# One step of a two-layer delta-rule and pooling decoder: memory keys moved to the front, x scaled before its split, ScalarE evictions, and a finer weave

## The chip, the core and the metric

The kernel is one program on one core of a Trainium2 chip. The metric is device time in microseconds (us) from the first to the last instruction of the program, as the median of several runs; one more execution was taken with the hardware profiler, and all rows below come from it. The engines are PE (TensorE, matrix products, 128x128 array), DVE (VectorE), ACT (ScalarE), POOL (GpSimd) and SP (SyncE, which here only issues transfers). SBUF is the on-chip memory with 128 partitions, PSUM the eight banks into which PE writes.

## The reference, cut to what matters

A prompt of 256 tokens and eight decode sequences of four tokens (288 columns together) go through two layers, all in float32. Layer 0 mixes with a gated delta rule of 12 heads, layer 1 with causal pooling; each also has four heads that attend to 256 memory tokens. Then comes a dense SwiGLU feed-forward network. The parts that the change touches:

```
def rmsnorm(x, w):
    y = xf * lax.rsqrt(jnp.mean(xf * xf, axis=-1, keepdims=True) + EPS)
    return (y * w).astype(x.dtype)

mkv = [mem_kv(mem_prompt, norm_mem[l], w_mem_kv[l]) for l in range(DEPTH)]   # memory keys and values
h = rmsnorm(x, norm_mix[l])
proj = h @ w_in                                   # q|k|v, z, a, b, q_mem of layer 0
qkv, conv_new = causal_conv(qkv, conv_buf, conv_w)            # width 4, then silu
# delta rule, in chunks: lmat is strictly lower triangular, (eye + lmat) is solved
sol = lax.linalg.triangular_solve(eye + lmat, rhs, left_side=True, lower=True, unit_diagonal=True)
u = uv_c - wk_c @ S;  o = qg_c @ S + attn_c @ u;  S = S * gend_c + kend_c^T @ u
o = rmsnorm(o, onorm_w) * jax.nn.silu(z)
y_mem = cross_attn(q_mem, mem_k[l], mem_v[l])
x = x + jnp.concatenate([y_tok, y_mem], axis=-1) @ w_out[l]
x = x + swiglu(rmsnorm(x, norm_ffn[l]), w_gate_up[l], w_down[l])
```

## The kernel before

Activations lie transposed: 16 blocks of 128 features by 288 tokens. Every large product is made from two halves of each operand: `split` writes a rounded part `hi` (ACT) and the rest `lo` (DVE, `lo = src - hi`), and PE multiplies hi by hi, hi by lo and lo by hi. Weights come from DRAM in chunks of 512 KB through three `wraw` buffers (`wchunk`, L114), ACT makes `whi` (L130) and DVE `wlo` (L131) in pieces of 512 columns. `gemm_steps` (L144) is a generator: each step takes one chunk, which is 24 products of 128x128 by 288 columns, and collects up to four output blocks in the four `acc` banks of PSUM. When a block is done, `on_block` takes it out. Everything else that PE writes goes to four `aux` banks.

A framework records the instructions and orders them: program order gives the priority, and a simulated schedule made ahead of time picks, for each engine, the ready instruction of the highest priority. At run time each engine's queue is in order, and an instruction that waits holds all behind it. `tc.high_priority` moves an instruction ahead.

The stages follow one another so: x and the first key and query projection (`first = kq(0)`, L1154), with x's blocks (`x_block`) loaded between its chunks; then the constants, the rows of x for its norm (`x_norm`, L347, through `wraw` buffers), and the gates (`alpha_beta`, `rates`, `decays`). Since the norm of x comes late, x is split unscaled, and each projection is multiplied by the row `rs0` when it leaves PSUM, on DVE (L667, L670, L652, L714). Then the memory keys and values of layer 0 (`mem_kv`, L271; 192 products of 128x128 by 512 columns). Then six units of two heads each. `Unit.keys` makes the triangular inverse of a unit in levels of 2, 4, 8, 16, 32 and 64 (L848 to L943), `Unit.values` (L975) applies it, updates the states and normalizes. `drain(*gens)` (L476) takes one step of each generator in turn, so that the steps of `values(n)`, `keys(n + 1)`, the memory attention and the projections of the next units alternate: one step of the delta rule, one whole chunk. After that come the output projection (`out_proj`), the feed-forward network (`ffn`), layer 1 (`mix1`) with its own `mem_kv` and `attention`, its output projection, and the second `ffn`.

In `attention`, each pair of decode sequences copies its four probabilities' columns into a zero-padded tile `pad` (L454, POOL) from which PE multiplies (L457); `pad` has one set of columns for both values of b.

Of the kernel before, what the change touches and what calls it, by code (L numbers as in the profile page):

```python
# [16 lines left out]
P = 128  # L17
# [8 lines left out]
TS = 4  # L26
# [19 lines left out]
FILL = 48  # L46
# [6 lines left out]
def VZ(n):  # L53
    return [24 + 2 * n, 25 + 2 * n] + ([36 + 2 * n, 37 + 2 * n] if n < 5 else [])
# [3 lines left out]
def body(ctx: ExitStack, tc: tile.TileContext, i: dict, o: dict):  # L58
# [14 lines left out]

    def acc():
        return accp.tile([P, 512], F32, name="acc", tag="acc", bufs=4)
# [9 lines left out]
    nc.sync.dma_start(cols[:, :32], i["cols"][:, :32])  # L85
# [58 lines left out]
    def gemm_steps(chunk, ncols, kt, act, on_block, ks=2, order=None, bank=None, parts=1):  # L144
# [4 lines left out]
        for k0 in order:  # L149
            nk = min(ks, kt - k0)  # L150
            w = wchunk(chunk(k0 // ks), nk, ncols, parts=parts if k0 == 0 else 1)
            last = k0 == order[-1]
            kj = [(k, j) for k in range(nk) for j in range(nb)]
            for k, j in sorted(kj, key=lambda t: t[1]) if last else kj:
# [4 lines left out]
                en = last and k == nk - 1  # L159
                nc.tensor.matmul(pv, wh, xh, start=st, stop=False)  # L160
                nc.tensor.matmul(pv, wh, xl, start=False, stop=False)  # L161
                nc.tensor.matmul(pv, wl, xh, start=False, stop=en)  # L162
                if en:
                    on_block(j, pv)
            yield
# [14 lines left out]
    class Norm:  # L180
# [25 lines left out]
        def rstd(self):  # L206
            ps = aux()
            for t in range(3):
                rows = P if t < 2 else NS
                nc.tensor.matmul(  # L210
# [19 lines left out]
    def spread_psum(r):  # L230

        ps = aux()
        for t in range(3):
            rows = P if t < 2 else NS
            nc.tensor.matmul(  # L235
# [8 lines left out]
    def row_squares(src, rows, out):  # L244

        for h in range(2):
            t = wpool.tile([P, 1024], F32, name="rows", tag="wraw", bufs=3)[:rows]
            nc.sync.dma_start(t, src[:, h * 1024 : (h + 1) * 1024])
            nc.scalar.activation(t, t, AF.Square, accum_out=out[:rows, h : h + 1])

    def mem_norm():
        q = sp.tile([P, 2, 2], F32, name="mq", tag="mq", bufs=1)
        for t in range(2):
            row_squares(i["mr"][t * P : (t + 1) * P], P, q[:, t])
        mss = small(2, "mss", bufs=1)
        nc.vector.tensor_tensor(mss, q[:, :, 0], q[:, :, 1], op=ALU.add)
# [14 lines left out]
    def mem_kv(l, mem, part_tile, half, kt_, v_):  # L271
        mt = []
        pss = [[acc() for _ in range(2)] for _ in range(2)]
        for k0 in range(0, KT, 2):
            for k in (k0, k0 + 1):
                mt.append(split(mem(k), memw(l, k), hi=part_tile(), lo=part_tile()))
            for part in range(2):
                w = wchunk(i["wkv"][l, part, k0 // 2], 2, 512)
                for t in range(2):
                    for k in range(2):  # L280
# [5 lines left out]
                        nc.tensor.matmul(pv, xh, w[k][0], start=st, stop=False)  # L286
                        nc.tensor.matmul(pv, xl, w[k][0], start=False, stop=False)
                        nc.tensor.matmul(pv, xh, w[k][1], start=False, stop=en)  # L288
                yield
        for t in range(2):  # L290
# [11 lines left out]
            for h in range(NMH):  # L302
                nc.tensor.transpose(
# [8 lines left out]
    pad = cp.tile([P, 2, NMH, 2 * SHIFT + TS], F32, name="pad")  # L312
# [26 lines left out]
    rs0 = sp.tile([P, NT], F32, name="rs0", tag="rs0", bufs=1)  # L339

    def load_constants():
        nc.sync.dma_start(ident, i["ident"])
        nc.sync.dma_start(masks, i["masks"])
        nc.sync.dma_start(levels, i["levels"])
        nc.sync.dma_start(cols[:, 32:], i["cols"][:, 32:])

    def x_norm():  # L347
        q = sp.tile([P, 3, 2], F32, name="xq", tag="xq", bufs=1)
        for t in range(3):
            rows = P if t < 2 else NS  # L350
            row_squares(i["xr"][t * P : t * P + rows], rows, q[:, t])
        ss = small(3, "xss", bufs=1)
        nc.vector.tensor_tensor(ss[:, :2], q[:, :2, 0], q[:, :2, 1], op=ALU.add)
        nc.vector.tensor_tensor(ss[:NS, 2:], q[:NS, 2:, 0], q[:NS, 2:, 1], op=ALU.add)
# [3 lines left out]
    def attention(l, ys, g2, s4, ahead):  # L358
        y = ys[NH:]
        for h in range(NMH):  # L360
            ps = aux()
            pv = ps.rearrange("p (t m) -> p t m", t=2)
            for t in range(2):
                nc.tensor.matmul(
# [13 lines left out]
            for t in range(2):  # L378
                nc.vector.tensor_scalar(e[:, t, :], e[:, t, :], sm[:, t : t + 1], None, op0=ALU.mult)
            pt = aux()  # L380
            ptv = pt.rearrange("p (m t) -> p m t", m=2)
            for m in range(2):
                for t in range(2):
                    nc.tensor.transpose(
# [3 lines left out]
            nc.vector.tensor_copy(pT, ptv)  # L388
            po = aux()
            for m in range(2):  # L390
                nc.tensor.matmul(
# [4 lines left out]
            yield  # L396
# [19 lines left out]
        for b0 in range(0, B, 2):  # L416
            ps = aux()
            for b in (b0, b0 + 1):
                ktb = loaded.pop(0)
                fetch()  # L420
                for h in range(NMH):
                    nc.gpsimd.tensor_copy(
                        pad[:, b % 2, h, SHIFT : SHIFT + TS],
                        y[h][:, NP + b * TS : NP + (b + 1) * TS],
                    )
                for h in range(NMH):
                    nc.tensor.matmul(
                        ps[32 * h : 32 * h + 32, :NM], pad[:, b % 2, h, cols(b)], ktb[:, h, :],
# [1143 lines left out]
```

## Time and profile before

| | us |
|---|---|
| median of three runs (2725.65 to 2731.15) | 2729.69 |
| the profiled execution | 2727.26 |
| its span | 2725.5 |
| PE busy in it | 2657.4 (98%) |
| DVE / ACT / POOL busy | 1593.0 / 1237.9 / 316.5 |

The time of the profiled execution is 1.8 us more than its span. PE's busy time counts pipelined products whose ends are modelled, so it tells where PE had nothing to do, and not how fast it ran; for that the column of the granted clock is read, which is 1.00 at 2.4 GHz and 0.50 at 1.2 GHz.

### The profile page before, as it was taken

The numbers are of one execution on the slowest core, as the hardware profiler recorded it, in microseconds if no ns is written. First come the engines' busy times: TensorE is split into PE (matmuls) and PEld (weight loads), VectorE is DVE, ScalarE is ACT, GpSimd is POOL, SyncE is SP. The second block draws the span as 40 slices with busy tenths as digits, with TensorE's granted clock in tenths as the row PEclk, the third lists the DMA queues.
The fourth block names the chain that finished last, engine by engine and source line by source line (L and its number), as shares of the span: only waits on it lengthen the run. The fifth ranks groups of instructions, "written<-read, shape, count | busy, mean of one in ns | idle before, by whom it ended". The sixth has DMA issues, their size and how long they took to land. (4 is left out here: it accounts for less than half of the span.)

```text
span 2725.5 us, 54445 instructions
## 1 busy us (share of the span) xinstructions
PE 2657.4 (98%) x21400; PEld 2571.2 (94%) x21400; DVE 1593.0 (58%) x3178; ACT 1237.9 (45%) x2407; POOL 316.5 (12%) x620
## 2 busy tenths in 40 slices
PE   7899999999999999999999999999999999999998
PEld 6888888788999999999999988899999999999997
DVE  5558776777655555445555566766555544555544
ACT  5454444444544444344444454455444433444443
POOL 0103221221101000000010111111001000001000
PEclk8999999999999999999999999999999999999998
DMA  7374345434545445455554575655455544545453
GB/s 255 122 233 134 102 151 171 143 118 169 164 164 169 167 166 168 165 169 165 170 166 167 166 248 160 216 174 162 164 170 164 169 167 166 167 166 170 164 170 128
DMA packets 133424, 455.86 MB, mean 167 GB/s; under 512 B 19440, under 2 KB 22000, under 8 KB 133168
## 3 DMA queue, kind: packets, MB, share of 16 engines
q1 hardware_dynamic: 133168, 452.38, 50.1%
q8 instruction: 168, 2.75, 0.4%
q14 instruction: 88, 0.72, 0.1%
HBM read 439.46 MB, written 12.86 MB: 166 GB/s over the span
## 5 line engine op out<-in xcount | busy, mean ns | idle before, releaser
L131 DVE TENSOR_TENSOR wlo<-wraw,whi 128x512 fp32r<-128x512 f32 (+1 forms) x1548 | 1066.6, 696 | 976.7 <-ACT whi L130 946.7
L130 ACT CAST whi<-wraw 128x512 fp32r<-128x512 f32 (+1 forms) x1548 | 939.7, 614 | 1214.2 <-PE acc L161 1128.4
L160 PE MATMUL acc<-a,whi 128*128 128x288 f32 x4864 | 1445.0, 297 | 19.0 <-ACT whi L130 19.0
L162 PE MATMUL acc<-a,wlo 128*128 128x288 f32 x4864 | 1443.8, 297 | 0.0
L161 PE MATMUL acc<-a,whi 128*128 128x288 f32 x4864 | 1443.4, 297 | 0.0
L160 PEld LDWEIGHTS acc<-a,whi 128*128 128x128 f32 x4864 | 918.6, 189 | 24.8 <-ACT whi L130 20.2
L162 PEld LDWEIGHTS acc<-a,wlo 128*128 128x128 f32 x4864 | 918.2, 189 | 5.6 <-issue 2.4
L161 PEld LDWEIGHTS acc<-a,whi 128*128 128x128 f32 x4864 | 918.9, 189 | 3.9 <-issue 1.4
L160 PE MATMUL acc<-b,whi 128*128 128x288 f32 x960 | 282.3, 294 | 0.0
L162 PE MATMUL acc<-b,wlo 128*128 128x288 f32 x960 | 282.3, 294 | 0.0
L161 PE MATMUL acc<-b,whi 128*128 128x288 f32 x960 | 282.3, 294 | 0.0
L1227 POOL TENSOR_TENSOR b<-b,rrow 128x288 f32<-128x288 f32 x88 | 89.4, 1034 | 1259.8 <-ACT b L1226 1259.8
L160 PEld LDWEIGHTS acc<-b,whi 128*128 128x128 f32 x960 | 180.1, 188 | 0.0
L162 PEld LDWEIGHTS acc<-b,wlo 128*128 128x128 f32 x960 | 180.1, 188 | 0.0
L161 PEld LDWEIGHTS acc<-b,whi 128*128 128x128 f32 x960 | 180.1, 188 | 0.0
L195 POOL TENSOR_TENSOR ssum<-ssum,sq 128x288 f32<-128x288 f32 x56 | 53.0, 947 | 427.6 <-ACT sq L194 425.6
L286 PE MATMUL acc<-whi,a 128*128 128x512 f32 x128 | 50.9, 406 | 5.1 <-ACT a L174 5.1
L288 PE MATMUL acc<-wlo,a 128*128 128x512 f32 x128 | 50.2, 393 | 0.0
L1225 DVE TENSOR_TENSOR b<-acc,rrow 128x288 f32<-128x288 f32 x88 | 40.1, 456 | 16.1 <-PE acc L162 16.1
L1226 ACT ACTIVATE b<-b 128x288 f32<-128x288 f32 x88 | 36.6, 439 | 26.1 <-DVE b L1225 25.8
L1231 DVE TENSOR_TENSOR b<-acc,b 128x288 f32<-128x288 f32 x88 | 39.9, 454 | 1.6
L690 DVE SCALAR_TENSOR_TENSOR ckq<-xp,cols,ckq 128x312 f32<-128x312 f32 x72 | 37.2, 547 | 0.7 <-ACT ckq L688 0.5
(378 smaller groups left out, 1607.0 us busy)
## 6 DMA issues: line engine op xcount, KB each, us to landing
wraw<-in_wgu_dram SPq DMA_DIRECT2D x352, 512.0 KB, 3.3
wraw<-in_wdn_dram SPq DMA_DIRECT2D x176, 512.0 KB, 3.2
wraw<-in_w_dram SPq DMA_DIRECT2D x103, 512.0 KB, 3.7
wraw<-in_wout_dram SPq DMA_DIRECT2D x64, 512.0 KB, 3.3
wraw<-in_wkv_dram SPq DMA_DIRECT2D x32, 512.0 KB, 4.2
wraw<-in_w1u_dram SPq DMA_DIRECT2D x32, 384.0 KB, 3.2
s<-in_dS_dram SPq DMA_DIRECT2D x12, 512.0 KB, 4.8
out_dram<-s SPq DMA_DIRECT2D x12, 512.0 KB, 3.8
```

The costliest lines, as they stand in the source:

```text
L130: nc.scalar.copy(hi[:, :n], src)
L131: nc.vector.tensor_tensor(lo[:, :n], src, hi[:, :n].bitcast(F32), op=ALU.subtract)
L160: nc.tensor.matmul(pv, wh, xh, start=st, stop=False)
L161: nc.tensor.matmul(pv, wh, xl, start=False, stop=False)
L162: nc.tensor.matmul(pv, wl, xh, start=False, stop=en)
L195: nc.gpsimd.tensor_tensor(self.sum, self.sum, q, op=ALU.add)
L286: nc.tensor.matmul(pv, xh, w[k][0], start=st, stop=False)
L288: nc.tensor.matmul(pv, xh, w[k][1], start=False, stop=en)
L690: nc.vector.scalar_tensor_tensor(c[:, :312], xp[:, q : q + 312], convw(q, f), c[:, :312], op0=ALU.mult, op1=ALU.add,)
L1225: nc.vector.tensor_tensor(t, ps, rs, op=ALU.mult)
L1227: nc.gpsimd.tensor_tensor(t, t, rs, op=ALU.mult)
L1231: nc.vector.tensor_tensor(t, ps, t, op=ALU.mult)
```

## The change

Five things, with much renaming around them (`nc.tensor.matmul` becomes `mm`).

1. The order at the start. `mem_kv` of layer 0 runs first; x's rows, x's blocks, the memory's rows (`mem_norm`), the constants and the gates are placed between its steps. The rows go through buffers of their own (`gp`, four of 256 KB) instead of `wraw`.
2. `rs0` is ready before x is split, so `x_block` multiplies x by it, and the projections leave PSUM by a plain copy on ACT (z straight through Silu).
3. Further work moves from DVE to ACT: the keys' transposes, the scaling of v, part of the output's, the last copy of the inverse, the scaling and the copy of the attention's probabilities.
4. The eight `copy_predicated` on 32 partitions at the start of each inverse become four of double width; for that `la` of both halves is one tile.
5. `gemm_steps` yields twice in a chunk. `Lane` and `weave` take the place of `drain(*gens)`: the number that a generator yields is how many half chunks pass before its next step. z gets projections of its own, which are moved to later units; ten half chunks of the output projection are the filler of the last unit. In `values` the four state multiplies on POOL stand behind the state's products; `pad` gets a second set.

```
-    def drain(*gens):
-        live = list(gens)
-        while live:
-            for g in list(live):
-                if next(g, live) is live:
-                    live.remove(g)
+    class Lane:
+        def __init__(self, gen, wait=0):
+            self.gen, self.at, self.live = gen, wait, True
+        def go(self, now):
+            while self.live and self.at <= now:
+                n = next(self.gen, self)
+                if n is self:
+                    self.live = False
+                else:
+                    self.at = now + max(1, n or 1)
+    def weave(filler, lanes, side=None):
+        now, more = 0, True
+        if side:
+            side.at = 0
+        while more or any(t.live for t in lanes):
+            for t in lanes + ([side] if side else []):
+                t.go(now)
+            if more:
+                more = next(filler, lanes) is not lanes
+            now += 1
...
+                n += 1
+                if n % max(1, len(kj) // 2) == 0:
+                    yield
...
-                    nc.vector.tensor_tensor(y[h], ps, rs0, op=ALU.mult)
-                nc.scalar.activation(y[h], y[h], AF.Silu)
+                    nc.scalar.activation(y[h], ps, AF.Silu)
...
-                    nc.vector.tensor_tensor(
-                        xp[:, 3:259], ps[:, :NP], rs0[:, :NP], op=ALU.mult
-                    )
-                    nc.vector.tensor_tensor(
-                        xs[:, :, 3:7], s4v(ps[:, NP:]), s4v(rs0[:, NP:]), op=ALU.mult
-                    )
+                    nc.scalar.copy(xp[:, 3:259], ps[:, :NP])
+                    nc.scalar.copy(xs[:, :, 3:7], s4v(ps[:, NP:]))
...
                 for q in range(4):
-                    for t in range(2):
-                        cp_(
-                            uc[bl(q), 2 * t : 2 * t + 2, :], mask(1, bl(q), 2),
-                            la[t][bl(q), :, 0, bl(q)],
-                        )
+                    cp_(
+                        uc[bl(q), 0:4, :].rearrange("p (t h) c -> p t h c", t=2),
+                        lev[1][bl(q)].unsqueeze(1).unsqueeze(1).broadcast_to([32, 2, 2, 32]),
+                        la["all"][bl(q), :, :, 0, bl(q)],
+                    )
...
                     nc.scalar.copy(yc[:, 0:4], pY[:, 0:4])
...
+                    yield 1
...
-                    yield
+                    yield 2
...
+                for hh in range(2):
+                    for c in range(2):
+                        sc_ = s0[hh][:, 4 * c : 4 * c + 4, :]
+                        gt(sc_, sc_, gends[...], op=ALU.mult)
...
             nc.sync.dma_start(t, i["xT"][:, k0:k1])
+            tt(t, t, rs0.unsqueeze(1).broadcast_to([P, k1 - k0, NT]), op=ALU.mult)
...
-        first = kq(0)
-        x_block(0)
-        next(first)
-        for n in range(1, 6):
+        mem = mem_kv(0, mem_blocks(ck), lambda: at(F32R)[:, :NM], ga, KT_, V_)
+        steps(mem, 8)
+        nc.sync.dma_start(ident, i["ident"])
+        nc.sync.dma_start(cols[:, :64], i["cols"][:, :64])
+        nc.sync.dma_start(cols[:, 80:], i["cols"][:, 80:])
+        xq = x_rows(gp)
+        steps(mem, 6)
+        x_norm(xq)
+        wab = gp([P, 512]).rearrange("p (k c) -> p k c", c=32)
+        nc.sync.dma_start(wab, i["wab"])
+        for n in range(6):
             x_block(n)
-            next(first)
+            steps(mem, 2)
+            if n == 2:
+                mem_norm(gp)
         load_constants()
...
+        steps(mem, 7)
+        ab = alpha_beta(wab)
+        drain(mem)
+        z = lambda n: project(72 + 4 * n, [36 + 2 * n, 37 + 2 * n])
...
+        weave(kq(0), [Lane(begin(), 1)])
+        weave(chain(kq(1), vb_(0), z(0)), [Lane(units[0].keys(), 4)])
...
+            filler = (
+                chain(kq(2), vb_(1), project_q()) if n == 0
+                else chain(kq(n + 2), z(n), vb_(n + 1)) if n < 4
+                else chain(z(4), vb_(5), z(5)) if n == 4 else take(out, 10)
+            )
+            weave(filler, lanes, att if 1 <= n < 4 else None)
```

## Rows read from the trace of the kernel before

**Rows 1.** The page: span, and busy time of the engines.
```profile
span 2725.5 us, 54445 instructions
PE 2657.4 (98%) x21400; PEld 2571.2 (94%) x21400; DVE 1593.0 (58%) x3178; ACT 1237.9 (45%) x2407; POOL 316.5 (12%) x620
```

**Rows 2.** Windows by stage: length, busy us per engine, clock, DMA share, GB/s.
```profile
0.00:60.00 60.00, 41.00 (x284) 37.58 (x285) 26.34 (x69) 28.70 (x55) 3.97 (x32) 0.86 0.81 261
60.00:130.00 70.00, 65.89 (x726) 60.40 (x726) 47.13 (x157) 34.14 (x80) 12.93 (x36) 0.98 0.38 119
130.00:150.00 20.00, 16.03 (x71) 13.26 (x70) 11.96 (x34) 11.13 (x22) 2.11 (x8) 0.83 0.77 237
...
210.00:660.00 450.00, 427.38 (x4540) 379.53 (x4539) 340.63 (x921) 203.42 (x523) 121.41 (x280) 0.97 0.42 137
660.00:1700.00 1040.00, 1038.30 (x7710) 1025.40 (x7709) 577.74 (x978) 473.55 (x854) 90.07 (x141) 1.00 0.52 172
1700.00:1760.00 60.00, 57.05 (x515) 50.47 (x515) 41.56 (x108) 26.05 (x59) 11.95 (x42) 0.97 0.67 221
```

**Rows 3.** Waits of PE, whole run: total us, times, longest us.
```profile
PE acc L160 <- ACT whi L130: 19.0, 2, 12.4
PE aux L860 <- DVE h L852: 6.9, 6, 2.3
PE acc L286 <- ACT a L174: 5.1, 2, 4.0
PE aux L457 <- POOL pad L454: 4.8, 3, 2.6
PE aux L1025 <- DVE ag L434: 3.3, 1, 3.3
...
PE aux L1035 <- DVE v L1032: 2.8, 2, 1.8
```

**Rows 4.** SP's queue, 14 to 60 us: start, us, instruction.
```profile
17.20 6.65 SPq L1162 DMA_DIRECT2D alog<-in_a_log_dram  x1
...
24.43 9.43 SPq L248 DMA_DIRECT2D rows<-in_xr_dram  x6
36.84 0.35 SPq L120 DMA_DIRECT2D wraw<-in_w_dram  x1
```

**Rows 5.** Transfers issued, whole run: count, KB each, us to landing.
```profile
wraw<-in_wkv_dram SPq DMA_DIRECT2D x32, 512.0 KB, 4.2
```

**Rows 6.** Narrow windows, columns as in rows 2.
```profile
10.00:20.00 10.00, 10.00 (x68) 10.00 (x67) 7.54 (x16) 6.98 (x16) 0.00 (x0) 1.00 0.99 338
20.00:30.00 10.00, 8.83 (x68) 8.60 (x66) 3.53 (x8) 2.68 (x7) 0.49 (x3) 1.00 0.80 142
...
160.00:180.00 20.00, 20.00 (x90) 16.57 (x89) 12.18 (x21) 10.72 (x20) 0.00 (x0) 1.00 0.74 247
...
400.00:410.00 10.00, 6.68 (x45) 5.28 (x44) 8.79 (x24) 1.40 (x3) 8.01 (x23) 0.78 0.76 271
...
550.00:560.00 10.00, 10.00 (x78) 10.00 (x77) 4.47 (x7) 3.89 (x7) 0.00 (x0) 1.00 0.46 162
```

**Rows 7.** DVE by line, 60 to 660 us: count, busy us, mean ns, idle before.
```profile
L841 DVE COPY_PREDICATED uc<-levels,u 32x64 f32<-32x64 uint8 x48 | 15.5, 358 | 0.3
L667 DVE TENSOR_TENSOR xp<-acc,rs 128x256 f32<-128x256 f32 x33 | 13.7, 417 | 0.4 <-PE acc L162 0.3
...
L670 DVE TENSOR_TENSOR xp<-acc,rs 128x32 f32<-128x32 f32 x33 | 5.9, 178 | 0.0
```

**Rows 8.** ACT by line, 60 to 660 us, columns as in rows 7.
```profile
L653 ACT ACT_TABLE_LOAD x5 | 6.4, 1283 | 0.1
...
L395 ACT COPY a<-aux 128x256 f32<-128x256 f32 x4 | 1.5, 368 | 3.1 <-PE aux L391 3.1
```

**Rows 9.** DVE in order of time, 396 to 404 us.
```profile
399.95 4.48 DVE L105 TENSOR_SCALAR c12y<-ssq 128x12 int32<-128x12 int32 x1
```

**Rows 10.** POOL in order of time, 396 to 410 us.
```profile
400.34 4.06 POOL L1104 TENSOR_TENSOR s<-s,gends 128x512 f32<-128x512 f32 x4
```

More of the change, by code (lines that the diff above doesn't have):

```diff
@@ L151, in gemm_steps @@
             w = wchunk(chunk(k0 // ks), nk, ncols, parts=parts if k0 == 0 else 1)
[L152 removed]
+            last_ = k0 == order[-1]
             kj = [(k, j) for k in range(nk) for j in range(nb)]
[L154 removed]
+            if last_:
+                kj.sort(key=lambda t: t[1])
+            n = 0
+            for k, j in kj:
                 pv = pss[j][:, :NT]
@@ L476, in drain, with steps @@
     def drain(*gens):
-        live = list(gens)
-        while live:
-            for g in list(live):
-                if next(g, live) is live:
-                    live.remove(g)
+        for g in gens:
+            for _ in g:
+                pass
+    def steps(g, n):
+        for _ in range(n):
+            next(g, None)
     def take(g, n):
@@ L486, in take, with out_proj, load, on @@
             yield
-    def steps(g, n):
-        for _ in range(n):
-            next(g, None)
+    class Lane:
[18 more added lines that the diff above has]
+            now += 1
+    def out_proj(l, order, after, ys=None):
+        ys = {} if ys is None else ys
+        def load(g, c):
+            p = order.index(c)
+            for k in (2 * q + n for q in order[p : p + 2] for n in range(2)):
+                if k not in ys:
+                    ys[k] = split(y[k])
+            return i["wout"][l, g, c]
+        for g in range(4):
+            def on(j, ps):
+                k = 4 * g + j
+                nc.vector.tensor_tensor(x[k], x[k], ps, op=ALU.add)
+                after(k)
+            yield from gemm_steps(
+                lambda c: load(g, c), 512, KT, lambda k: ys[k], on,
+                order=[2 * c for c in order],
+            )
     y = [None] * 16
@@ L760, in keys @@
                     )
-                for hh in range(2):
-                    for t in range(3):
-                        rows = P if t < 2 else NS
-                        n = t * 2 + hh
-                        nc.tensor.matmul(
-                            pq[:rows, n : n + 1], q2[hh][:, t * P : t * P + rows], ones[:, 0:1],
-                            start=True, stop=True,
-                        )
                 ts = nc.vector.tensor_scalar
@@ L797, in keys @@
                         )
+                    for hh in range(2):
+                        ts_ = slice(t * P, (t + 1) * P)
                         n = t * 2 + hh
@@ L811, in keys @@
                     )
+                for hh in range(2):
                     for m, sc in ((0, nrb), (1, rk)):
@@ L1062, in values @@
                     mm(H(pz[:NS], hh), selq[:, hh], rs, start=False, stop=True)
+                pe = aux()
+                for hh in range(2):
+                    mm(H(pe, hh), kend[:, 1, hh, :], u[1][:, hh, :], start=True, stop=True)
                 on = v2([P, 4, P])
@@ L1192, in body @@
         nc.sync.dma_start(x4[g], i["xT"][:, 4 * g : 4 * g + 4])
[L1193 to L1212 removed]
+    x += [x4[k // 4][:, k % 4] for k in range(KT)]
     def ffn(l, nrm, fp, nbuf, after):
@@ L1283, in body @@
         queries = gemm_steps(lambda c: i["w1q"][c], 512, KT, n2.act, on_q)
-        steps(queries, 6)
+        steps(queries, 12)
         rs1 = n2.rstd()
@@ L1366, in body @@
         )
-        steps(out, 5)
+        steps(out, 8)
         drain(group(1, aux))
         drain(group(0, aux))
-        steps(out, 4)
+        steps(out, 8)
         nc.sync.dma_start(o["pool"], st)
```

351 lines of the change are left out of this document (169 added, 182 removed).

## The prediction

> **What bounds the kernel now.** I read the page first. PE is busy for 2657.4 of 2725.5 us [rows 1], and the change takes no product away from it; so what can be won is the 68 us in which PE is idle, and the time in which it runs at 1.2 GHz. The second view is the windows by stage. For each stage I take two numbers: the idle time (length less PE's busy time) and the clock loss ((1 - clock) times length). The reader should see that the long stage of feed-forward and output products from 660 to 1700 us loses 1.7 us in 1040, and that almost everything lies ahead of 660 us [rows 2]. The third view, PE's waits, says for whom PE stood: two waits of together 19.0 us for the weights' cast, so 12.4 and 6.6; one of 4.0 us at the memory projection; then many short ones behind DVE in the triangular levels and in the values [rows 3].
>
> There are three places.
>
> *The start.* From 0 to 60 us PE idles 19.0 us and the clock costs 8.4 us, some of it inside the gap of 12.4 us, where it costs nothing: I count 5. SP's queue explains the gap: the broadcast of `alog` holds SP for 6.65 us, behind it stand the six transfers of x's rows for 9.43 us, and the next weight chunk is issued at 36.8 us [rows 4]. From 130 to 150 us PE idles 4.0 us (the first split of the memory) and the clock costs 3.4, of which I count 2. Together 24 + 6 = 30 us [rows 2, 3].
>
> *The delta rule.* From 60 to 130 and from 210 to 660 us PE idles 4.1 + 22.6 = 26.7 us, and the clock costs 1.4 + 13.5 = 14.9 us: 41.6 us. DVE is busy 76% of the second stretch, ACT 45% [rows 2]. The load is uneven: DVE has 8.8 of 10 us in the window with the stall of 3.3 us, and 4.5 in a window where only projections run [rows 3, 6].
>
> *Layer 1.* From 1700 to 1760 us PE idles 3.0 us and the clock costs 1.8 [rows 2]. The longest wait for `pad` is 2.6 us [rows 3].
>
> **The start, costed.** The work of the memory's 192 products doesn't change: 90 of that kind take 20 us [rows 6], so 222 ns each, 42.7 us. What changes is the bytes that must land before the last of them. By the shapes and the order of the code all of this is issued before it: 16 weight chunks of 512 KB (half of the 32 that both layers load [rows 5]), the memory twice (2048 KB each), x twice (2304 KB each), and 1435 KB of constants and the gates' weights. That is 18.3 thousand KB, 18.8 MB. The first 60 us of before moved 261 GB/s at a share of 0.81 [rows 2], so 322 GB/s of busy engines, constants with their small packets included; 18.8 MB take 58 us. With 2 us ahead of the first transfer (an estimate: the first product starts at 6.6 us, after transfer, cast and table load), 2 us for the last cast and split, and 2.7 us for the last 12 products, the memory part ends at about 65 us. PE has 42.7 us of work in it: 22 us are lost. Before, PE spent these bytes' time on projections that need fewer bytes for each product, and had its memory work later. So the new start is bound by transfers, and the gain is 30 - 22 = 8 us, less than the gap of 12.4 us suggests.
>
> The first product at half clock costs the same in both. Bounds: if the 6.65 us hold of SP stops the transfers and the low clock costs its 5 us again, the loss is 34 and the gain -4. If the transfers run at 338 GB/s throughout [rows 6], 3 us less, and the gates' products fill a few gaps, the gain is 13.
>
> **The delta rule, costed.** DVE sheds the two multiplications of each convolved block, 13.7 + 5.9 us, and half of the 48 `copy_predicated`, 7.7 us of 15.5 [rows 7]: 27 us of the 388 in the two stretches, 7%. I take a copy of double width as no longer than one of before. Several smaller moves (transposes, v, the output's scaling) come on top and I leave them out of the sum. ACT gets 33 pairs of copies; by its 368 ns for 128x256 from PSUM [rows 8], and no more for the narrow one, at most 24 us: it goes from 237.5 to 262 of 520 us, 50%. Where cover is gone: a copy on ACT now frees the bank, see the rivals.
>
> The weave matters more. A half chunk is 12 products, and 78 take 10 us [rows 6], so 1.5 us. `keys` now asks for 28 half chunks and `values` for 8 + 22 = 30, of 32 in a unit's filler; before, both had whole chunks one by one and were through after about ten of sixteen. So the delta rule's work on DVE is spread over the whole unit, and each dependent product has filler put ahead of it by order and not only by the schedule's guess. Where DVE is late by 1 to 2 us, as in most of the waits [rows 3], this covers it.
>
> What it doesn't cover is shown by the worst case. A DVE instruction on 12 columns took 4.48 us while POOL ran four state multiplications in 4.06 us [rows 9, 10], and the stall of 3.3 us follows it [rows 3]. The change keeps these four together in each unit. `values` has three half chunks (4.6 us) behind them, but the next unit's `keys` stands in its levels then, with one or two (1.5 to 3.1 us). So up to 4.1 - 1.5 = 2.6 us may stay in each of six units, 16 us; I take half, 8. Of the other 33 us I take 10 as staying. The gain is 41.6 - 18 = 24 us. Bounds: 3 us if only DVE's 7% helps; 36 us if nearly all goes.
>
> The Trainium skill (SBUF — State Buffer, "SBUF: two separate sides") says that DVE and POOL share one pair of ports as an exclusive lock, held for a whole instruction, and that the loser blocks fully. The trace agrees (4.48 us beside 4.06 us). By that rule alone all of the 16 us would stay and the time would be 8 us longer than my sum; by the rows, only what exceeds the filler.
>
> **Layer 1.** With two sets, the copy into `pad` no longer waits for the products that read the first. The 2.6 us go, and the clock's 1.8 us that follow: 4 us. Bounds 0 and 5.
>
> **The rest at nothing.** The ten half chunks of the output projection in the last unit were already available to the schedule as filler; a stall there is one of the 41.6 us. The new splits of y are ACT and DVE work beside products that keep PE full, as from 660 to 1700 us [rows 2]; without that cover each would cost its own time once. x's six scalings lie in the transfer-bound start.
>
> **Sum.** 8 + 24 + 4 = 36 us from the profiled execution's 2727.3 us gives 2691. That execution is 2.4 us below the median of the runs, 2729.7, so I predict a median of 2694 us, and take the rivals' gains from 2729.7 too.
>
> **The rivals.**
>
> *A. The start gains nothing* (0.17). The gain is -4 instead of 8: 2706 us. For it: transfers set the pace and the constants stand ahead of the last three half steps of the memory weights. Against it: x's rows no longer occupy `wraw`, so three chunks, 8 us of products, can be in flight while SP is held.
>
> *B. The weave gains little* (0.17). The waits came from single late instructions, not from crowding, and the finer order is undone by the schedule, which reorders anyway: 6 instead of 24, so 2712 us. For it: the 4.48 us instruction. Against it: DVE's 88% around the stall and 45% elsewhere.
>
> *C. ACT holds the banks; slower* (0.09). Each of 19 projections (six of keys, of values and of z, one of queries) now leaves through ACT's queue. In the last chunk the blocks close one after another, 6 products or 0.8 us each, so of four the first bank has 2.3 us until the next projection wants it. A copy takes 0.4 us and its narrow one some 0.2; if more than 1.7 us of casts, convolutions and table loads (1.28 us each [rows 8]) stand ahead, PE waits. At 1.9 us of waiting per projection the 36 us are gone; at 2.3 us the time is 2694 + 44 = 2738 us. Against it: ACT is at half load, and the copies are marked ahead of other work.
>
> A finer weave may also alternate Silu and Exp more often. With four more table loads in each of six units ACT would have 24 x 1.28 = 31 us more, 56% in all. The Trainium skill (ScalarE: Activation LUTs, "What ACT_TABLE_LOAD costs") gives 1283 ns for the load, which the trace shows, and a further 1380 ns of draining, which no run here shows; by it the estimate is 64 us, and ACT at 63%.
>
> *D. A and B together* (0.05). -4 + 6 + 4 = 6 us: 2724 us, no change.
>
> **How the numbers follow.** My forecast has 0.52: 2694, with its own range from 2676 (all best bounds, 13 + 36 + 5) to 2706. A measurement of this kernel can tell some 0.2%, 5.5 us, from no change. Faster: forecast, A and B, 0.86; the same: D, 0.05; slower: C, 0.09. The range for 8 in 10 takes in A and B with some room above, and at the lower end the small moves that I left out: 2668 to 2722 us. Outside are C, D and a tail below.
>
> **What would show it.** Start: the first memory product near 6.6 us, the last near 65 us, transfers at a share above 0.85 until then, no single gap of 12 us; if the memory part ends by 55 us, my bytes are wrong; if after 75 us, A. Delta rule: idle plus clock loss up to the end of the units near 18 us, DVE without windows above 0.85, fewer waits at the levels' products; one stall per unit next to POOL's four multiplications if the ports are the limit; waits of projections' first products for ACT's copies if C. Layer 1: no wait of over 1 us for `pad`. The prediction is wrong if PE's busy time itself grows, or if the loss comes back at a place that had none, such as the output projection waiting for x.

## The result, and the profile after

The changed kernel takes 2702.51 us (median of 4 runs, 2699.17 to 2704.79); the kernel before, run beside it, 2730.42 (2725.65 to 2732.71). The ratio is 0.9899, 95% interval 0.9885 to 0.9913: faster by 28 us. The prediction was 2694 us, with a range of 2668 to 2722: the direction and the range hold, and the forecast gain of 36 us was 8 us too large. A second series of the same changed kernel (the control below) gave 0.9888; where an experiment is set against "the changed kernel" below, it is against the middle of the two, 0.9894, or for the last four against the control on the same chip.

The page of after, to be set against [rows 1]. PE's busy time falls by 12.7 us; DVE's falls by 45.7 us (1593.0 to 1547.3) and ACT's grows by 42.9:

```profile
span 2697.4 us, 54395 instructions
PE 2644.7 (98%) x21400; PEld 2557.9 (95%) x21400; DVE 1547.3 (57%) x3016; ACT 1280.8 (47%) x2583; POOL 327.1 (12%) x620
```

PE's work is the same 21400 products. That its busy time falls fits the granted clock: the clock losses in the table below fall by 12.6 us. The windows by stage, cut where the stages now lie (columns as in [rows 2]):

```profile
0.00:80.00 80.00, 63.86 (x288) 44.87 (x288) 47.36 (x108) 51.06 (x116) 3.50 (x26) 0.96 0.85 272
80.00:100.00 20.00, 20.00 (x152) 19.64 (x152) 13.11 (x50) 7.99 (x17) 0.00 (x0) 1.00 0.89 308
100.00:150.00 50.00, 48.06 (x472) 46.29 (x471) 37.43 (x99) 33.59 (x85) 15.88 (x46) 0.97 0.46 145
150.00:650.00 500.00, 484.91 (x5201) 439.40 (x5200) 333.19 (x852) 262.47 (x700) 137.09 (x291) 0.99 0.45 146
650.00:1665.00 1015.00, 1013.46 (x7523) 1002.18 (x7522) 558.70 (x938) 466.20 (x837) 83.75 (x128) 1.00 0.52 171
1665.00:1735.00 70.00, 66.06 (x585) 58.58 (x583) 48.66 (x130) 32.21 (x74) 14.29 (x55) 0.98 0.63 211
1735.00:2697.00 962.00, 948.41 (x7193) 946.93 (x7191) 508.90 (x841) 427.23 (x757) 72.63 (x74) 0.99 0.49 165
```

Idle time (length less PE's busy time) and clock loss ((1 - clock) times length), by stage, in us; in brackets first the idle time, then the clock loss. The clock has two digits, so its loss in the 500 us of the units is good to some 2.5 us:

| stage | lost before | lost after | gain | forecast |
|---|---|---|---|---|
| start with memory part | 30 (19.0 + 4.0; 5 + 2) | 19.3 (16.1 + 3.2) | 10.7 | 8 |
| delta rule | 41.6 (26.7 + 14.9) | 23.5 (1.9 + 15.1; 1.5 + 5.0) | 18.1 | 24 |
| layer 1's attention | 4.8 (3.0 + 1.8) | 5.3 (3.9 + 1.4) | -0.5 | 4 |
| long stage and tail, idle alone | 14.9 (1.7 + 13.2) | 15.1 (1.5 + 13.6) | -0.2 | 0 |

The gains add up to 28.1 us, and the spans differ by 2725.5 - 2697.4 = 28.1 us.

PE's waits from 0 to 70 us, and then from 70 us to the end (total us, times, longest us), to be set against [rows 3]:

```profile
PE acc L294 <- ACT whi L132: 11.9, 2, 7.4
PE aux L666 <- ACT a L181: 3.2, 1, 3.2
```

```profile
PE aux L917 <- DVE h L909: 7.0, 4, 1.9
PE aux L470 <- DMA s<-in_cv_dram: 3.2, 3, 2.1
...
PE aux L970 <- DVE h L966: 2.5, 3, 1.1
PE acc L165 <- DVE x L544: 1.9, 1, 1.9
PE aux L960 <- DVE h L949: 1.5, 3, 0.6
...
PE acc L165 <- ACT xp L726: 0.2, 1, 0.2
```

At the start two waits for casts of the weights are left: the first product's, 7.4 us, and one of 4.4 us from 21.8 to 26.2 us, where the kernel before had 12.4. The wait of 4.0 us at the memory's split is gone; one of 3.2 us for a split of x, ahead of the gates' products (L666), is new. In the delta rule the stall of 3.3 us is gone. What is left in the delta rule is a handful of waits of under 2 us, the largest group at the first of the triangular levels (L917). A projection's first product (L165) waits for ACT's copy out of PSUM (L726) for 0.2 us in the whole run. The waits for `pad` are replaced by waits for the transfers of `cv`.

### The profile page after: what moved, and what is told of

Read it like the earlier page. It is cut to its first block, busy times and chain, and to the rows that moved or that the text cites. A ratio compares the mean times of both kernels' runs of the same rounds, so it can differ in the third digit from the quotient of the medians.

```text
span 2697.4 us, 54395 instructions
## 1 busy us (share of the span) xinstructions
PE 2644.7 (98%) x21400; PEld 2557.9 (95%) x21400; DVE 1547.3 (57%) x3016; ACT 1280.8 (47%) x2583; POOL 327.1 (12%) x620
## 4 chain that ended last, share of the span: by engine, by line
PE 93%; DVE 3%; ACT 1%; DMA 1%; issue 1%; POOL 0%; SPq 0%; DVEq 0%; ACTq 0%; POOLq 0%
PE acc L165 28%; PE acc L166 28%; PE acc L167 28%; DVE wlo L133 1%; PE acc L294 1%; PE acc L295 1%; PE acc L296 1%; ACT whi L132 1%; DMA wraw<-in_wkv_dram 0%; PE aux L934 0%; PE aux L917 0%; PE aux L438 0%; PE aux L812 0%; PE aux L1076 0%; PE aux L1185 0%
## 5 line engine op out<-in xcount | busy, mean ns | idle before, releaser
L133 DVE TENSOR_TENSOR wlo<-wraw,whi 128x512 fp32r<-128x512 f32 (+1 forms) x1548 | 1081.0, 705 | 994.1 <-ACT whi L132 970.5
L165 PE MATMUL acc<-a,whi 128*128 128x288 f32 x4864 | 1442.5, 297 | 3.1 <-DVE x L544 1.9
L165 PEld LDWEIGHTS acc<-a,whi 128*128 128x128 f32 x4864 | 913.3, 188 | 11.1 <-issue 2.8
L165 PE MATMUL acc<-b,whi 128*128 128x288 f32 x960 | 282.1, 294 | 0.0
L165 PEld LDWEIGHTS acc<-b,whi 128*128 128x128 f32 x960 | 180.1, 188 | 0.0
L1289 DVE TENSOR_TENSOR b<-acc,rrow 128x288 f32<-128x288 f32 x88 | 40.1, 456 | 16.1 <-PE acc L167 16.1
L294 PEld LDWEIGHTS acc<-whi,a 128*128 128x128 f32 x128 | 24.8, 197 | 22.1 <-ACT whi L132 13.4
```

What stands on the lines that cost most here:

```text
L133: nc.vector.tensor_tensor(lo[:, :n], src, hi[:, :n].bitcast(F32), op=ALU.subtract)
L165: mm(pv, wh, xh, start=st, stop=False)
L294: mm(pv, xh, w[k][0], start=st, stop=False)
L1289: nc.vector.tensor_tensor(t, ps, rs, op=ALU.mult)
```

## The experiments

### Undo the spacing, undo the moves, and both

*e1, whole chunks again*: lanes advance once per whole chunk, the waits ahead of the lanes are 0, and `z` stands ahead of the key and query blocks as before.

```
-                    self.at = now + max(1, n or 1)
+                    n = max(1, n or 1)
+                    self.at = now + ((2 if n > 1 else 0) if self.even else n)
...
-            lanes = [Lane(units[n].values(), 0 if n == 5 else 8)]
+            lanes = [Lane(units[n].values(), 0, True)]
```

> The changed kernel with the old spacing: any two steps of keys and values one whole chunk apart, started at once, the new small yields without effect (z of a unit ahead of the next keys' projection, since the values now end earlier). If the spacing is what covered PE's waits, the idle time and clock loss of the delta rule (22 us in the changed kernel, 41.6 us before) go back to 35 to 42 us, and the time is 13 to 20 us above the changed kernel's 2702.5: ratio to before about 0.996. If the relief of DVE did it, the loss stays below 28 us and the ratio below 0.993.

Measured: 2715.77 us, ratio 0.9953 (0.9938 to 0.9968), so 0.0059 or 16 us slower than the changed kernel. The window of the units, and the largest of PE's waits from 90 to 670 us:

```profile
150.00:650.00 500.00, 475.77 (x4962) 430.20 (x4961) 324.16 (x830) 254.07 (x681) 131.74 (x286) 0.98 0.44 139
```

```profile
PE aux L918 <- DVE h L910: 17.2, 5, 3.8
```

PE idles 24.2 us there instead of 15.1, and the clock is at 0.98 instead of 0.99. The wait at the first level is 17.2 us instead of 7.0 (the lines are shifted by one). So the spacing covers late DVE instructions at the first level above all.

*e2, the moved copies and scalings of the delta rule back to DVE*, all else as changed. One of six such edits:

```
-                    nc.scalar.copy(xp[:, 3:259], ps[:, :NP])
-                    nc.scalar.copy(xs[:, :, 3:7], s4v(ps[:, NP:]))
+                    nc.vector.tensor_copy(xp[:, 3:259], ps[:, :NP])
+                    nc.vector.tensor_copy(xs[:, :, 3:7], s4v(ps[:, NP:]))
```

> The changed kernel with the work of the delta rule that went to ACT put back on DVE (convolved blocks' and queries' copies out of PSUM, keys' transposes, v's and the output's scaling, one copy of the inverse); the spacing stays. If DVE's relief is what gained, DVE's busy time from 100 to 650 us rises by some 45 us and PE's loss there from 22 to above 33 us: ratio to before 0.994 or more. If the spacing alone gained, the loss stays within 5 us of 22: ratio 0.990 to 0.992.

Measured: 2713.1 us, ratio 0.9944 (0.9929 to 0.9959), 14 us slower than the changed kernel. The same window, and the two largest waits:

```profile
150.00:650.00 500.00, 477.99 (x5124) 429.77 (x5123) 353.42 (x932) 232.16 (x580) 128.59 (x289) 0.98 0.45 142
```

```profile
PE aux L960 <- DVE h L949: 5.6, 3, 1.9
PE aux L917 <- DVE h L909: 5.5, 5, 1.9
```

DVE has 20 us more work in 500, ACT 30 less; from 100 to 650 us DVE has 25 us more, where I expected some 45. The new wait is at the next level (L960), where it was 1.5 us.

*e5, both of these edits together*, the memory part and all else as changed.

> The changed kernel with the spacing of the first experiment and the DVE work of the second undone together. One at a time they cost 13 and 11 us. If each covers the same late instructions by another means, both undone lose no more than some 20 us, since the waits are counted once: ratio to before 0.996 to 0.998. If they are independent, or each needs the other, the losses add or more: 24 us or above, ratio 0.999 and up, and what is left of the gain is the start's.

Measured: 2717.11 us (9 runs, the kernel before in 12), ratio 0.9959 (0.9946 to 0.9971). Alone the edits lose 16 and 14 us, together 0.0065 or 18, not 30. So the spacing is worth some 4 us when the work is back on DVE, and the lighter DVE some 2 us when the spacing is gone, neither clear of nothing: each needs the other, and neither is worth much alone. My expectation had this the wrong way round: two remedies of which either would do lose little one at a time and much together. What is left against before is 0.0041 of 2727, 11 us. Its windows:

```profile
0.00:80.00 80.00, 61.30 (x274) 43.19 (x275) 45.76 (x106) 50.92 (x116) 2.98 (x26) 0.94 0.82 267
100.00:150.00 50.00, 49.56 (x601) 46.58 (x600) 40.44 (x117) 29.04 (x66) 13.45 (x42) 1.00 0.48 144
150.00:650.00 500.00, 477.81 (x4972) 429.20 (x4970) 352.56 (x923) 228.56 (x572) 134.05 (x293) 0.98 0.44 138
```

The start loses 23.5 us in this execution (other runs with the same start 18.5 to 21.7), the delta rule 32.6. Before, they lost 30 and 41.6. So the 11 us aren't the start's alone: some 9 us, good to 2.5, were won in the delta rule with both edits undone. A candidate is named below, under the port.

### The start

*e4, two steps of the memory part between the three lots of x's rows.*

```
-        xq = x_rows(gp)
-        steps(mem, 6)
+        xq = x_rows(gp, lambda: steps(mem, 2))
```

> The changed kernel with the twelve transfers of x's rows issued in three lots with two steps of the memory projection after each, in place of all twelve and then six steps; same bytes, same sums. If transfers bound the start as predicted, the end of the memory part (77 us) moves by less than 2 us and so does the time. If SP was held by the four row buffers, which ACT has to free, so that weight chunks were issued late (the gap from 20 to 26 us), the gap of 7.4 us shrinks and the time falls by 3 to 6 us: ratio 0.988.

Measured: 2702.89 us, ratio 0.9907 (0.9892 to 0.9921), no change; the transposes behind the memory's products begin at 77.0 us, as in the changed kernel. PE's waits up to 70 us:

```profile
PE acc L294 <- ACT whi L132: 9.5, 2, 7.6
PE aux L667 <- ACT a L181: 4.2, 1, 4.2
```

The first product's wait is 7.6 us of the 9.5 (my expectation took the 7.4 us for the gap). So the gap itself falls from 4.4 to 1.9 us: part of it came from SP, which had to wait ahead of the rows' transfers. But the wait at the gates grows from 3.2 to 4.2 us, the clock up to 80 us is 0.94 instead of 0.96, and the part ends as late as before. This order of the transfers doesn't matter for the end.

*e7, the constants behind the memory part's last chunks* (`steps(mem, 7)` ahead of `load_constants()`).

> The changed kernel with the constants (masks, levels, convolution states, the two broadcasts, one of which holds SP for 7.2 us) issued after the memory's last weight chunks in place of ahead of the last three. If transfers bound the start, the memory part ends 3 to 5 us earlier (the bytes and the hold move behind it) but the first keys' projection gets its chunks later by as much: time within 3 us of 2702.5, ratio 0.989 to 0.991. If the hold itself starves PE, the time falls by 4 us or more: ratio 0.988.

Measured: 2701.22 us, ratio 0.9900 (0.9878 to 0.9923), the memory's end 0.9 us earlier, where 3 to 5 us were expected: 980 KB, 3.1 us at 322 GB/s, moved behind the part and did little for its end, though SP no longer holds the last chunks for `alog`. The total doesn't change, as expected. In the changed kernel PE is busy without a break from 57.4 us to the part's end, so what comes after the chunk that it had then hardly counts.

*e8, fewer bytes.* Three quarters of the transfers of the memory's rows are left out (1536 KB); the squares of the first quarter stand for the others, so the memory's keys and values are scaled wrongly.

```
-            t = tile_([P, 512])[:rows]
-            nc.sync.dma_start(t, src[:, h * 512 : (h + 1) * 512])
+            if h == 0 or few is False:
+                t = tile_([P, 512])[:rows]
+                nc.sync.dma_start(t, src[:, h * 512 : (h + 1) * 512])
```

> The changed kernel without three quarters of the transfers of the memory's rows: the sums of squares of the memory's norm are taken four times from the first 512 columns, so the memory keys and values are scaled wrongly; ScalarE's work is the same. 1536 KB less, 4.9 us at 322 GB/s. If bytes set the pace of the start, the memory part ends 4 to 5 us earlier and the time falls by that: ratio 0.988. If buffers, SP's order or ScalarE set it, nothing changes: 0.990.

Measured: 2699.17 us, ratio 0.9894 (0.9875 to 0.9913). The transposes at the end of the memory part, first in the changed kernel, then here (ns minimum, median, maximum; first and last start):

```profile
L311 PE MATMUL aux<-ident,ag x8: 270/272/273, 77.0 to 77.8; 128*128 128x128 f32 x8
```

```profile
L315 PE MATMUL aux<-ident,ag x8: 272/272/328, 72.5 to 73.3; 128*128 128x128 f32 x8
```

They come 4.5 us earlier; 1536 KB (1.57 MB) at 322 GB/s are 4.9 us. That fits a start that goes by its bytes. But the edit takes away more than bytes: the rows pass through four buffers that ACT has to empty, and SP waits less for them. SP's waits for these buffers from 0 to 80 us (total us, times, longest us), in the changed kernel and here:

```profile
SPq L255 <- ACT u L256: 17.5, 13, 5.6
```

```profile
SPq L256 <- ACT u L257: 8.7, 8, 3.7
```

Bytes and these waits aren't told apart, and e7 speaks against bytes alone. Shown is that without these transfers the memory part ends earlier; the total's interval holds both a gain of 5 us and none.

*e6, the memory part back behind the values and `z`*; x's rows, norm and scaling come first, spacing and moves as changed.

```
-            steps(mem, 2)
-            if n == 2:
-                mem_norm(gp)
+            steps(first, 2)
...
+        def mem_part():
+            mem_norm(gp)
+            yield from mem_kv(0, mem_blocks(ck), lambda: at(F32R)[:, :NM], ga, KT_, V_)
...
+        weave(chain(vb_(0), z(0), mem_part(), kq(1)), [Lane(units[0].keys(), 4)])
```

> The changed kernel with the memory keys in their old place (between the first z projection and the second keys' projection) and x's rows, norm and scaled blocks at the start. My theory: the start's gain came from taking the memory's transfers and x's norm together, so here PE starts late (rows, norm and scaling first: first product at 15 to 20 us in place of 7.4) but then projections need fewer bytes, and the memory part runs without a gap; the loss up to the end of the memory part is 20 to 26 us against 19.5 plus 3, so the time is 0 to 6 us above 2702.5: ratio 0.990 to 0.992. The rival, that memory first is worth the whole start's gain: ratio 0.994 or more.

Measured: 2710.73 us, ratio 0.9936 (0.9917 to 0.9956), 0.0042 or 11 us slower than the changed kernel. My theory's 0 to 6 us missed it; the rival's 0.994 lies in the interval. PE's waits up to 60 us:

```profile
PE aux L242 <- DVE c3y L113: 22.4, 1, 22.4
```

The first product of all now stands behind x's norm for 22.4 us, 15 more than the first product's 7.4 in the changed kernel. This is what "memory first" saves in this kernel, 11 us of the total: x is scaled ahead of its split, nothing of x can start before its norm, and the memory's products are the only ones that need no norm. In the kernel before x's norm wasn't in that way.

### Layer 1, the first level, and what is left

*e3, the sample part of layer 1's attention at half pace.*

```
+        def slow(g):
+            for n, k in enumerate(g):
+                yield k if n < 12 else 2 * k
...
-            [Lane(attention(1, y, ga, s4, 3), 3)],
+            [Lane(slow(attention(1, y, ga, s4, 3)), 3)],
```

> The changed kernel with the sample part of layer 1's attention at half the pace (twice the half chunks between its steps). In the changed kernel PE waits 3.2 us there for the values' transfers and the clock falls once, 5.6 us of loss from 1665 to 1735 us. If the faster steps outran the transfers, both go: loss 1 us or less, time 4 to 5 us below 2702.5, ratio 0.988. If the wait has another cause (the three buffers, whatever the pace), nothing changes: 0.990.

Measured: 2702.2 us, ratio 0.9903 (0.9886 to 0.9919): no change in the total, where 4 to 5 us were expected. The stage, in the changed kernel and here:

```profile
1660.00:1740.00 80.00, 75.75 (x651) 67.59 (x651) 55.83 (x149) 38.36 (x89) 15.51 (x59) 0.98 0.60 202
```

```profile
1660.00:1740.00 80.00, 78.84 (x690) 71.40 (x689) 60.51 (x162) 41.02 (x94) 17.46 (x64) 1.00 0.63 210
```

Locally the loss falls from 4.3 + 1.6 to 1.2 + 0 us, and no wait for `cv` remains. But this profiled execution reached layer 1 8.4 us later (the memory's transposes of layer 1 ended at 1630.4 instead of 1622.0 us), with more falls of the clock ahead of it, though nothing ahead of layer 1 was changed. It ended 3.9 us later, so 4.5 us were won behind that point. The total can't show it; e10 speaks for it.

*e9, the first level later in `keys`*: seven half chunks instead of five ahead of it, in every unit but the last.

```
-                yield 5
+                yield 7 if h0 < 10 else 5
```

> The changed kernel with two more half chunks ahead of the first level of the inverse (7 in place of 5, units 0 to 4). In the changed kernel PE's largest remaining wait there is for DVE's transpose of that level, 7.0 us in four waits of up to 1.9 us. If too little spacing is left at this place, these waits go (below 2 us in all), with the clock's falls beside two of them: 5 to 8 us, ratio 0.987 to 0.988. If the schedule, which is made ahead, only puts other work there and the wait moves, the time stays: 0.990.

Measured: 2697.3 us, ratio 0.9873 (0.9857 to 0.9890); the control on the same chip 0.9888, so 4 us faster, with intervals that overlap. The same window, and the largest wait:

```profile
150.00:650.00 500.00, 487.29 (x5253) 440.70 (x5252) 330.44 (x856) 264.73 (x702) 135.14 (x291) 0.99 0.45 146
```

```profile
PE aux L917 <- DVE h L909: 3.7, 3, 1.9
```

The wait at the level falls by 3.3 us, the stage's idle time by 2.4. Expected were a wait below 2 us and a gain of 5 to 8.

*e10, the edits of e9, e3 and e7 together.*

> The later first level, layer 1's slower attention and the constants behind the memory's last chunks together. If their local gains (5 to 8 us, 4.7 us in layer 1 by the third experiment's profile, 1 us at the memory's end) add up: 10 to 13 us below the control, ratio 0.9855 to 0.987. If the clock's falls elsewhere eat them up, ratio 0.989 or more.

Measured: 2693.68 us (2692.78 to 2695.3), ratio 0.9863 (0.9848 to 0.9878): 6.9 us below the control on the same chip, all four runs below the control's fastest (2698.73). It beats both kernels; the expected 10 to 13 us were too much. Its windows:

```profile
150.00:650.00 500.00, 488.03 (x5241) 442.60 (x5242) 331.52 (x853) 265.10 (x702) 134.15 (x287) 0.99 0.45 147
1660.00:1740.00 80.00, 77.47 (x679) 70.09 (x678) 56.95 (x152) 38.30 (x86) 15.49 (x58) 1.00 0.61 212
```

Idle time is 3.1 us less than in the changed kernel in the first stage and 1.7 in the second, where the clock gives 1.6 more: 6.4 of the 6.9 us.

*e11, the changed kernel once more*, the control for these four.

> The changed kernel as it is, timed again beside the others of this group: ratio to before 0.990, within 0.0015; its profile differs from the first one only in where the clock falls, by up to 5 us.

Measured: 2700.6 us (2698.73 to 2703.14), ratio 0.9888 (0.9874 to 0.9903).

*e12, eight predicated copies of single width*, all else as changed.

```
-                    cp_(
-                        uc[bl(q), 0:4, :].rearrange("p (t h) c -> p t h c", t=2),
...
+                    for t in range(2):
+                        cp_(
+                            uc[bl(q), 2 * t : 2 * t + 2, :], mask(1, bl(q), 2),
+                            la[t][bl(q), :, 0, bl(q)],
+                        )
```

> The changed kernel with the eight predicated copies of a unit in place of the four of double width. By the rows 48 copies take 358 ns each and the 24 wider ones 310: DVE has 10 us more in 550. If each us on this chain counts, the wait at the first level grows by some 1.5 us in each unit, 6 to 9 us in all: ratio 0.993. If the spacing covers it: below 3 us, ratio 0.990 to 0.991.

Measured: 2705.12 us (2698.14 to 2706.03), ratio 0.9899 (0.9884 to 0.9913), not to be told from the control. DVE by line, 80 to 650 us (count, busy us, mean ns, idle before), in the changed kernel and here:

```profile
L897 DVE COPY_PREDICATED uc<-levels,la 32x128 f32<-32x128 uint8 x24 | 7.2, 299 | 0.4
```

```profile
L898 DVE COPY_PREDICATED uc<-levels,la 32x64 f32<-32x64 uint8 x48 | 9.0, 222 | 0.4
```

A copy of double width takes 299 ns and one of single width 222. The merge saves DVE 1.8 us in six units.

## Why the prediction was right, and where its sizes were off

**The start: the transfers count, as said; its end misplaced.** I had the memory part end at 65 us and a loss of 22 us; it ended at 77 us, with a loss of 19.3. The busy rate was right: 272 GB/s at a share of 0.85 are 320 GB/s. The step that failed is the share of 1 behind it: 58 us at 0.85 are 68, 10 us later. Two windows in which the share falls short:

```profile
20.00:30.00 10.00, 5.55 (x19) 4.10 (x18) 3.28 (x11) 7.43 (x21) 0.00 (x0) 0.85 0.81 271
60.00:70.00 10.00, 10.00 (x55) 6.44 (x54) 6.03 (x20) 4.42 (x11) 1.01 (x3) 1.00 0.69 185
```

Why it falls short isn't shown; SP's waits for the row buffers (e8) are a candidate. In SP's queue (start, us) the broadcast still stands ahead of the last three chunks:

```profile
54.58 7.23 SPq L1237 DMA_DIRECT2D alog<-in_a_log_dram  x1
61.86 0.43 SPq L1238 DMA_DIRECT2D dtb<-in_dt_bias_dram  x1
62.38 1.33 SPq L122 DMA_DIRECT2D wraw<-in_wkv_dram  x3
```

So 36 products came behind it, not 12; but e7, without this order, ends the part only 0.9 us earlier. That the loss is smaller all the same is due to what PE did in between. The 64 products of the gates (L666) take 9.3 us, which I had counted only in the upper bound. The memory's products keep PE busy for some 50 us, not 42.7: those from 8 to 13 us and from 27 to 30 us begin 0.43 us apart instead of 0.23, and the table counts that as busy time. So the 8 us came near the 10.7 in part by luck. My own sign for rival A, an end behind 75 us, appeared without A's result: the end of the part is not the loss. The loss has to be read from PE's idle time, whatever PE does meanwhile. What I didn't see is what the order protects against: by e6 it is the wait for x's norm, 22.4 us, which would otherwise be new at the head of the kernel.

**The delta rule: the mechanism is right, the size was 24 and is 18.** Both halves of my argument, DVE's shed work and the order by half chunks, count (e1, e2). But I had let the half chunks cover the late instructions by themselves and given DVE's work a bound of 3 us alone; by e5 and e2 the half chunks without the lighter DVE are worth some 4 us. Two terms were wrong in size.

*The port, 8 us kept; the rows show none.* POOL still runs the four multiplications of the states together, now right behind the states' products. DVE and POOL in order of time, 201 to 208 us, in the changed kernel:

```profile
202.00 0.36 DVE L909 STREAM_TRANSPOSE h<-uc 128x192 f32<-128x192 f32 x1
202.29 0.20 DVE L1001 COPY u<-uc 32x192 f32<-32x192 f32 x1
204.65 1.34 DVE L133 TENSOR_TENSOR wlo<-wraw,whi 128x512 fp32r<-128x512 f32 x1 [2.16 <-ACT whi L132]
206.23 1.22 DVE L133 TENSOR_TENSOR wlo<-wraw,whi 128x512 fp32r<-128x512 f32 x1 [0.24 <-ACT whi L132]
```

```profile
202.38 4.52 POOL L1084 TENSOR_TENSOR s<-s,gends 128x512 f32<-128x512 f32 x4 [12.21 <-PE aux L1076]
```

The chain's transpose and copy are over when POOL begins, and beside POOL stand two splits of weights, 1.34 and 1.22 us instead of 0.69. Beside the other five groups stand mainly splits of weights, beside the last one also splits of y; from 0.3 us ahead of each group to 2 us behind it PE waits at most 0.2 us. The instruction on 12 columns that took 4.48 us [rows 9] takes 172 to 174 ns in all six units:

```profile
L107 DVE TENSOR_SCALAR c12y<-ssq x6: 172/173/174, 126.1 to 536.0; 128x12 int32<-128x12 int32 x6
```

I had placed the next unit's levels beside the multiplications; by the rows the weights' splits stand there. That is the step that failed: what stands beside the group.

I also overlooked that the kernel before had two such stalls. At 315 us an instruction whose median is 0.42 us took 2.87 beside three of POOL's multiplications, and PE waited 2.6 us for DVE's next instruction (DVE, POOL, and PE's wait from 313 to 321 us):

```profile
315.25 2.87 DVE L828 TENSOR_TENSOR kE<-h,kE 32x256 fp32r<-32x256 f32 x1 [1.02 <-ACT kE L827]
```

```profile
314.79 3.05 POOL L1104 TENSOR_TENSOR s<-s,gends 128x512 f32<-128x512 f32 x3
```

```profile
PE aux L794 <- DVE u L800: 2.6, 1, 2.6
```

With the stall of 3.3 us these are 5.9 us of PE's idle time. In the changed kernel, and in e1, e2 and e5 as well, neither instruction is held. So the new place of POOL's group may have won part of what e5 leaves; no run puts it back, and this isn't shown.

The Trainium skill (SBUF — State Buffer, "SBUF: two separate sides") says that when a DVE instruction and a POOL instruction both need the pair of ports that they share, the one that starts first gets it for the whole instruction and the other fully blocks. The traces agree in part: a split beside POOL is 0.5 to 0.65 us longer, and in the kernel before, three short instructions in a row beside another group took 0.97 us each, about as long as one of POOL's multiplications (1.04 us):

```profile
492.76 0.97 DVE L110 SCALAR_TENSOR_TENSOR c12t<-c12t,ssq 128x12 f32<-128x12 f32 x1
```

The 4.48 and 2.87 us went over several of them; what decides that stays open. The prediction took the group of four for one hold.

*The rest, 10 us kept; 23.5 are there.* The half chunks do not reach the first level far enough (L917, 7.0 us; e9 takes half of it away), and the clock takes 6.5 us by the windows. The step that failed is that the half chunks cover what is late by 1 to 2 us: at the first level the five ahead of it are too few.

**The shed work.** Half of the predicated copies was to save 7.7 us: it saved 1.8 (e12). Between before and after these copies fall by 8.3 us (15.5 to 7.2), but most of that isn't the merge. The copy's 358 ns of [rows 7] isn't its own price: with the same width and count it takes 222 ns in the new order. Why it was longer before wasn't tried. The moves that I left out of the sum more than make up for it in DVE's busy time, which falls by 45.7 us in all.

**Layer 1: 4 forecast, -0.5 measured.** The wait for `pad` went, as said, and the next thing that was late is one I didn't name: the transfers of `cv`. In SP's queue all eight are issued in one run of 13.6 us; before, they were spread from 1701.5 to 1735.5 us (the first and the last):

```profile
1675.28 13.56 SPq L419 DMA_DIRECT2D s<-in_cv_dram  x8
```

```profile
1701.51 0.37 SPq L408 DMA_DIRECT2D s<-in_cv_dram  x1
...
1735.19 0.33 SPq L408 DMA_DIRECT2D s<-in_cv_dram  x1
```

The reason is in the change: it also drops the helper that held this attention back, one step for three whole chunks, and most steps now stand two half chunks apart:

```
-            slowly(att),
+            [Lane(attention(1, y, ga, s4, 3), 3)],
```

So the attention outruns its transfers; at half the new pace they are hidden (e3, e10). That the pace had changed, and what would then be late next, is the step I left out.

**The rivals.** A: see above; the start gained more than forecast. B: refuted by the 18.1 us and e1, though without the lighter DVE the spacing is worth about what B gave it. D needs A and B, and neither came. C: refuted; a projection waits for ACT's copy for 0.2 us, and ACT's table loads from 80 to 650 us are 15 (7 + 6 + 1 + 1), as many as before from 60 to 660. The finer weave alternates Silu and Exp no more often.

**The sum.** 8 + 24 + 4 = 36 was forecast, 10.7 + 18.1 - 0.5 - 0.2 = 28.1 came. The errors partly cancel.

## What to carry to other kernels

Filler put between dependent steps and a lighter engine behind them are one remedy, not two: cost them together, and look at which step is still short of filler, since two more half chunks there (e9) took half of the largest wait away. When an order is changed so that a norm comes ahead of a split, ask what the first engine can do that needs no norm, and put that first. When a wait goes, name what the engine will wait for next (here a transfer), look whether the edit also changes the pace, and pace the work to it; and take the duration of a short instruction from a place where it runs undisturbed, not from a mean.

## What the runs showed of the hardware

The granted clock differs between executions of one kernel: in the control's four runs it was 0.994 at 2698.76 us and 0.990 at 2703.14. A short fall in the units looks like this, the changed kernel at 549 us (PE busy throughout, at 1.2 GHz for most of it):

```profile
549.00:553.00 4.00, 4.00 (x105) 3.20 (x91) 1.77 (x7) 0.27 (x1) 0.00 (x0) 0.57 0.49 181
```

At 0.57 it costs 0.43 x 4 = 1.7 us. Just ahead of it PE had waited 1.9 us for DVE (L917). The changed kernel's profile and the control's have such falls at the same places; that of e3, whose order of products is the same up to layer 1, has further ones, among them at 196 and 468 us, and was 8.4 us later by layer 1. What decides where they come, beyond the waits just ahead of some of them, stays open. So an edit worth under 5 us has to be read from its stage, as e3 and e8 were, and isn't proved by the total.
